# The framework's reordering is switched off around a kernel's own instruction planner

## The chip, the cores and the metric

The kernel runs on one core of one Trainium2 chip. The core has five engines with a queue of instructions each: TensorE (PE, matrix products and transposes; PEld in the profile is its weight load), VectorE (DVE), ScalarE (ACT), GpSimd (POOL) and SyncE (SP, which here only issues DMAs). Each engine runs its queue in the order in which the program holds it and stops where an instruction waits for another engine or for a DMA. The metric is the device time of one execution in microseconds, as the median over several runs.

## The reference, cut to what matters

Two layers of an encoder over 512 tokens of width 1024. Each layer has four steps, and after each a LayerNorm over the residual:

```python
for i in range(DEPTH):                      # DEPTH = 2
    y = swiglu(x, ffn_w_gate[i, 0], ffn_w_up[i, 0], ffn_w_down[i, 0])
    x = layer_norm(ALPHA * x + 0.5 * y, ln_g[i, 0], ln_b[i, 0])
    if i % 2 == 0:
        y = mixer_ab(x, ...)                # 8 heads full attention, 8 heads windowed with a sink
    else:
        y = mixer_c(x, ...)                 # 16 heads, 2-D neighbourhood attention with a bias table
    x = layer_norm(ALPHA * x + y, ln_g[i, 1], ln_b[i, 1])
    y = memory_attn(x, mem, ...)            # 4 heads of 256 into 256 memory tokens
    x = layer_norm(ALPHA * x + y, ln_g[i, 2], ln_b[i, 2])
    y = swiglu(x, ffn_w_gate[i, 1], ffn_w_up[i, 1], ffn_w_down[i, 1])
    x = layer_norm(ALPHA * x + 0.5 * y, ln_g[i, 3], ln_b[i, 3])
```

`swiglu` is `(silu(x @ w_gate) * (x @ w_up)) @ w_down` with a hidden width of 2816. All weights are float32, 217 MB read in all.

## The kernel before

**Products.** Every float32 operand is split into a high part (a cast to fp32r, on ACT) and a low part (the difference, on DVE): `split` (line 293). A product is then three matmuls, high by high, high by low and low by high: `mm3` (line 304). A weight piece of 128 x 1024 thus costs one DMA into a `raw` buffer (two of them), a cast on ACT and a subtraction on DVE into `slab` buffers (27 of them), and only then can PE use it. In the FFN, `down_fast` (line 505) saves one of eight products by sums and differences of blocks on DVE.

**Stages.** `run` (line 190) goes through eight steps: FFN 0, mixer A/B, memory attention, FFN 1, FFN 2, mixer C, memory attention, FFN 3. The activations stay in SBUF: `x` as four tiles of 128 tokens, and transposed and split as `xh` and `xl`, made by `to_features` (line 378: PE transposes into PSUM tiles `t`, ACT casts, DVE subtracts). PSUM tiles have the tags `a` (3), `d` (2) and `t` (3).

**The first FFN** begins by tokens: `ffn_by_tokens` (line 462) loads the first 128 tokens, transposes them, loads gate and up weights of 256 columns in halves, and does 48 matmuls of 256 columns for each token block, 24 into `a` (gate) and 24 into `d` (up). Between them it sets a condition: `self.nc.after = self.nc.ops[-1], {"scalar", "vector"}` (line 467) makes what ACT and DVE do on these weights wait, in the plan, for the last operation of `to_features(0)`. Similar conditions stand for SP's DMAs of side data: the masks `band` and `near` and the 16 `bias` tables (`bias_tables`, line 902, each a DRAM-to-DRAM copy of 128 KB) come after the last DMA of the first group of FFN 0 and FFN 1 (line 588), and the gains, rotary tables and sink of mixer A/B after the last DMA of FFN 0 (line 689). A condition of this kind is known to the planner alone; it is no dependency in the program.

**The planner.** `Graph` (line 64) stands in place of the engines while the kernel is written down: `record` (line 128) keeps each operation with its engine, its cost by a formula (`cost`, line 110) and the operations that it depends on. `emit` (line 165) then plays the program through: each engine has a clock, a heap of operations that will be ready and one of those that are; the operation that can start first is emitted, among the ready ones of an engine the one that was recorded first, and ACT and DVE ("patient") may wait a little for an earlier one. Tiles are granted in the order of recording as buffers come free. The real instruction is issued at that moment:

```python
            _, _, op = heapq.heappop(ready[e])
            op.call()
```

(lines 231 and 232). Line 140 makes that call, so all instructions have line 140 in the profile.

**The framework.** The instructions so emitted go to the framework's tile context (`tile.TileContext`, line 1283). On leaving the context it orders each engine's instructions anew: by its own estimate of times it lets an instruction that is ready pass one that is not, with the order of emission as the priority. It also places tiles in buffers and sets the semaphores.

Of the kernel before, what the change touches and what calls it, by code (L numbers as in the profile page):

```python
# [249 lines left out]
class Kernel:  # L250
# [939 lines left out]
    def run(self, phases=8):  # L1190
        nc, a = self.nc, self.a
        self.ident = self.tile(self.cst, [P, P], F32, "ident")
        make_identity(self.tc.nc, self.ident)
        self.xh = self.tile(self.big, [P, KB, S], F32R, "xh")
        self.xl = self.tile(self.big, [P, KB, S], F32R, "xl")
        self.x = []
        for t in range(NT):
            self.x.append(self.tile(self.big, [P, D], F32, f"x{t}"))
        self.nhalf = self.tile(self.cst, [P, 8], F32, "nhalf")
        nc.gpsimd.memset(self.nhalf, -0.5)  # L1200
        self.junk = self.tile(self.cst, [P, D], BF16, "junk")
        steps = [
            lambda last: self.ffn(0, 0, last, self.masks),
            lambda last: self.mixer_ab(1, last),
            lambda last: self.memory(0, 2, last),
            lambda last: self.ffn(1, 3, last, self.bias_tables),
            lambda last: self.ffn(2, 4, last),
            lambda last: self.mixer_c(5, last),
            lambda last: self.memory(1, 6, last),
            lambda last: self.ffn(3, 7, last),  # L1210
        ]
        for i in range(phases):
            steps[i](i == phases - 1)
        nc.emit()


@with_exitstack
# [69 lines left out]
```

## Time and profile before

| | us |
|---|---|
| median of three runs | 2249.43 (2248.94 to 2249.74) |
| profiled execution, its own time | 2250.06 |
| span of the profiled execution, first to last instruction | 2248.3 |

The page of the profile was taken from one execution. It names engines as above; line numbers are those of the kernel, and tiles have the names of the program without their numbers. In the rows of groups and of the timeline stands what an instruction writes and reads, its shape, how often, how long, and in brackets or behind the bar how long its engine stood idle before it and what ended that. In a row of a stretch (`from:to`) stand its length and then the busy time of each engine with the count of instructions.

### The profile page before, as it was taken

The page shows a single profiled execution, that of the slowest core. Times are in us where ns is not written, and L with a number is a line of the kernel's source. Part 1 is how long each engine was busy: PE and PEld are TensorE (multiplying, and loading weights), DVE is VectorE, ACT ScalarE, POOL GpSimd, SP SyncE. Part 2 cuts the span into 40 slices and gives each one's busy share as a digit, 9 for nine tenths or more (in the row PEclk, how much of TensorE's full clock was granted, in tenths as well). Part 3 has the DMA queues.
Part 4 walks back from the last instruction along what each step waited for, and adds up shares of the span by engine and source line. Part 5 has one row for each costly group of instructions (what it writes and reads, how often), then busy time and mean ns, then how long its engine had stood idle before and what let it go on. Part 6 is the DMA issues. An engine that isn't in the chain of part 4 may idle for free. (4 is left out here: it accounts for less than half of the span.)

```text
span 2248.3 us, 28157 instructions
## 1 busy us (share of the span) xinstructions
PE 2207.0 (98%) x11312; PEld 1871.7 (83%) x11312; DVE 1420.1 (63%) x2116; ACT 882.7 (39%) x1418; POOL 287.0 (13%) x391
## 2 busy tenths in 40 slices
PE   8999999999999999999999999999999999999998
PEld 7888888778898888888888888888888988888886
DVE  5666646788745766665655667368776457666653
ACT  4323332566433433333333333256554434333331
POOL 0000203543000100001100003013411001000011
PEclk9999999999999999999999999999999999999999
DMA  6333241003333332225312334212233333322241
GB/s 207 129 120 113 67 154 57 20 20 90 124 106 113 113 113 90 72 83 168 105 40 86 113 117 150 75 62 68 69 113 96 129 113 113 113 82 72 85 137 38
DMA packets 168755, 221.09 MB, mean 98 GB/s; under 512 B 6192, under 2 KB 136880, under 8 KB 168624
## 3 DMA queue, kind: packets, MB, share of 16 engines
q1 hardware_dynamic: 165552, 208.80, 28.9%
q0 software_dynamic: 3072, 10.49, 1.3%
q8 instruction: 89, 1.46, 0.3%
q14 instruction: 42, 0.34, 0.1%
HBM read 217.17 MB, written 4.19 MB: 98 GB/s over the span
## 5 line engine op out<-in xcount | busy, mean ns | idle before, releaser
L140 PE MATMUL a<-xh,slab 128*128 128x512 f32 (+1 forms) x2960 | 890.8, 382 | 0.0
L140 PEld LDWEIGHTS a<-xh,slab 128*128 128x128 f32 x2960 | 549.1, 188 | 107.1
L140 PE MATMUL d<-slab,slab 128*128 128x512 f32 (+2 forms) x2432 | 572.5, 384 | 4.7 <-DVE slab L140 2.8
L140 PE MATMUL a<-xl,slab 128*128 128x512 f32 (+1 forms) x1480 | 565.0, 382 | 0.0
L140 PEld LDWEIGHTS d<-slab,slab 128*128 128x128 f32 x2432 | 441.1, 188 | 94.3 <-DVE slab L140 4.2
L140 ACT CAST slab<-raw 128x1024 fp32r<-128x1024 f32 x316 | 320.7, 1050 | 310.9 <-DMA raw<-ffn_w_gate 129.8
L140 DVE TENSOR_TENSOR slab<-raw,slab 128x1024 fp32r<-128x1024 f32 x316 | 391.6, 1254 | 72.9 <-ACT slab L140 55.4
L140 PEld LDWEIGHTS a<-xl,slab 128*128 128x128 f32 x1480 | 278.3, 188 | 53.0
L140 DVE TENSOR_TENSOR slab<-slab,slab 128x1024 fp32r<-128x1024 f32 (+2 forms) x208 | 241.4, 1184 | 18.9 <-ACT slab L140 17.6
L140 ACT CAST slab<-slab 128x1024 fp32r<-128x1024 f32 (+1 forms) x144 | 140.1, 1000 | 238.4 <-DVE slab L140 238.3
L140 ACT CAST slab<-t 128x512 fp32r<-128x512 f32 (+3 forms) x261 | 143.5, 572 | 225.9 <-DVE t L140 142.0
L140 PE MATMUL a<-slab,slab 128*128 128x256 f32 (+3 forms) x1336 | 204.9, 303 | 6.2 <-DVE slab L140 2.6
L140 DVE TENSOR_TENSOR slab<-a,t 128x512 f32<-128x512 f32 x56 | 38.7, 691 | 269.3 <-PE a L140 269.3
L140 PEld LDWEIGHTS a<-slab,slab 128*128 128x128 f32 x1336 | 180.6, 194 | 21.5 <-DVE slab L140 6.0
L140 DVE TENSOR_TENSOR slab<-t,slab 128x512 fp32r<-128x512 f32 (+3 forms) x261 | 164.3, 654 | 42.7 <-ACT slab L140 41.5
L140 DVE SCALAR_TENSOR_TENSOR x<-d,x 128x512 f32<-128x512 f32 x216 | 147.3, 685 | 48.3 <-PE d L140 47.3
L140 PE MATMUL t<-slab,slab 128*128 128x512 f32 (+1 forms) x648 | 152.1, 379 | 0.0
L140 ACT ACTIVATE t<-a 128x512 f32<-128x512 f32 (+2 forms) x104 | 57.4, 552 | 225.2 <-PE a L140 203.0
L140 POOL TENSOR_TENSOR x<-x,slab 128x512 f32<-128x512 f32 x24 | 46.0, 1950 | 780.7 <-DVE x L140 780.7
L140 PEld LDWEIGHTS t<-slab,slab 128*128 128x128 f32 x648 | 115.7, 188 | 25.0 <-DVE slab L140 2.2
L140 POOL TENSOR_TENSOR t<-t,l 128x256 f32<-128x256 f32 (+2 forms) x104 | 80.1, 785 | 308.4 <-DVE l L140 308.4
L140 PE MATMUL a<-slab,xh 128*128 128x256 f32 (+1 forms) x432 | 98.1, 319 | 4.1 <-ACT xh L140 4.0
(97 smaller groups left out, 1810.0 us busy)
## 6 DMA issues: line engine op xcount, KB each, us to landing
raw<-ffn_w_gate SPq DMA_DIRECT2D x40, 1024.0 KB
raw<-ffn_w_up SPq DMA_DIRECT2D x40, 1024.0 KB
slab<-ffn_w_down SPq DMA_DIRECT2D x64, 512.0 KB
raw<-ffn_w_down SPq DMA_DIRECT2D x12, 1024.0 KB
raw<-mem_w_kv SPq DMA_DIRECT2D x8, 1024.0 KB
raw<-mem_w_kv SPq DMA_DIRECT2D x16, 512.0 KB
raw<-mem_w_q SPq DMA_DIRECT2D x8, 1024.0 KB
raw<-mem_w_o SPq DMA_DIRECT2D x8, 1024.0 KB
```

What stands on the lines that cost most here:

```text
L140: op.call = lambda: fn(*args, **kw)
```

## The change

Leaving the reordering out for everything that the planner emits: `manual_schedule` is the framework's context in which it keeps each engine's instructions in the order in which they are issued to it. Tiles, dependencies and semaphores are still the framework's. No operation is added, removed or changed.

```diff
@@ -1211,7 +1211,8 @@
         ]
         for i in range(phases):
             steps[i](i == phases - 1)
-        nc.emit()
+        with self.tc.manual_schedule():
+            nc.emit()
```

## The prediction

> **What bounds the kernel now.** The page comes first: which engine is busy over the whole span, and whether its clock is held back.
>
> ```profile
> span 2248.3 us, 28157 instructions
> PE 2207.0 (98%) x11312; PEld 1871.7 (83%) x11312; DVE 1420.1 (63%) x2116; ACT 882.7 (39%) x1418; POOL 287.0 (13%) x391
> PEclk9999999999999999999999999999999999999999
> ```
>
> TensorE (PE) works for 2207.0 of 2248.3 us at full granted clock, so only 41.3 us of the span are not its own work. The change adds and removes no instruction: it can win part of those 41.3 us, or make them more. The next view is the busy time by stretches (PE's first, then weight load, DVE, ACT, POOL, clock, DMA share, GB/s), cut where the idle time sits.
>
> ```profile
> 7.80:11.80 4.00, 0.00 (x0) 0.00 (x0) 2.94 (x3) 3.08 (x5) 0.00 (x0) 1.00 1.13 342
> 14.20:16.90 2.70, 2.69 (x13) 2.69 (x14) 0.66 (x1) 0.29 (x1) 0.00 (x0) 1.00 1.05 231
> 18.40:21.30 2.90, 2.90 (x26) 2.90 (x26) 0.00 (x0) 0.38 (x1) 0.00 (x0) 1.00 1.09 349
> 40.00:300.00 260.00, 260.00 (x1155) 214.88 (x1154) 167.31 (x196) 92.72 (x112) 12.73 (x8) 1.00 0.33 108
> 420.00:620.00 200.00, 191.89 (x1110) 162.08 (x1109) 158.19 (x358) 123.08 (x271) 65.88 (x107) 0.99 0.24 68
> 620.00:1480.00 860.00, 858.20 (x4230) 724.85 (x4229) 522.01 (x659) 299.54 (x411) 68.60 (x74) 1.00 0.31 101
> 1480.00:1740.00 260.00, 251.55 (x1563) 221.92 (x1562) 190.84 (x381) 145.14 (x305) 67.15 (x114) 0.99 0.27 86
> 1740.00:2222.00 482.00, 480.76 (x2433) 408.66 (x2432) 278.73 (x359) 166.40 (x236) 27.90 (x26) 1.00 0.30 99
> 2222.00:2249.00 27.00, 15.53 (x69) 12.53 (x67) 14.77 (x24) 4.97 (x8) 7.33 (x8) 0.88 0.29 78
> ```
>
> The long FFN stretches have nothing to give: 0 us idle in 40 to 300, 1.8 in 620 to 1480, 1.2 in 1740 to 2222. Four places remain: the start, the first token mixer with the memory attention's beginning (200 - 191.9 = 8.1 us), the second mixer (260 - 251.6 = 8.4 us), and the last 27 us, where the final LayerNorms and the output run one after another (11.5 us). The list of PE's waits (total, times, longest) says on whom it waited.
>
> ```profile
> PE t L140 <- DMA x<-x: 6.9, 2, 5.8
> PE a L140 <- ACT xh L140: 4.0, 1, 4.0
> PE t L140 <- DVE x L140: 3.1, 4, 1.2
> PE d L140 <- DVE slab L140: 2.8, 8, 0.7
> PE a L140 <- DVE slab L140: 2.6, 3, 1.2
> PE t L140 <- DVE slab L140: 2.5, 6, 0.6
> ```
>
> Two long waits belong to the start (5.8 us for the first DMA of x, 4.0 us for the cast xh). All others are short, none in these rows over 1.2 us.
>
> **How much order there is to change.** The program of before numbers its instructions as the planner emitted them, and runs them in another order. Laid side by side, from that program alone, 718 of 11312 matmuls stand elsewhere (394 by more than two places), 867 of 1956 DVE instructions (85), 414 of 1220 on ACT (42), and 158 of 299 DMAs on SP, up to 96 places. PE, which sets the time, thus keeps 94% of its order; its moved matmuls lie in the first 40 us and in the two mixers, with a few groups of 10 to 23 in the FFNs.
>
> **The start, the one term with a clear sign.** The timeline of the first 23 us, PE, then ACT, then DVE (start, us, instruction, idle time before it and what ended that):
>
> ```profile
> 5.83 1.94 PE L140 MATMUL t<-ident,x 128*128 128x128 f32 x8 [5.83 <-DMA x<-x]
> 11.81 0.80 PE L140 MATMUL a<-slab,xh 128*128 128x256 f32 x2 [4.04 <-ACT xh L140]
> 14.21 0.90 PE L140 MATMUL t<-ident,x 128*128 128x128 f32 x3 [1.04 <-DMA x<-x]
> 22.07 0.50 PE L140 MATMUL a<-slab,xh 128*128 128x256 f32 x2
> ...
> 7.22 1.04 ACT L140 CAST slab<-raw 128x1024 fp32r<-128x1024 f32 x1 [5.21 <-DMA raw<-ffn_w_gate]
> 8.73 1.04 ACT L140 CAST slab<-raw 128x1024 fp32r<-128x1024 f32 x1 [0.46 <-DMA raw<-ffn_w_gate]
> 10.23 1.04 ACT L140 CAST slab<-raw 128x1024 fp32r<-128x1024 f32 x1 [0.46 <-DMA raw<-ffn_w_up]
> 11.18 1.06 ACT L140 CAST xh<-t 128x512 fp32r<-128x512 f32 x2
> ...
> 9.80 1.23 DVE L140 TENSOR_TENSOR slab<-raw,slab 128x1024 fp32r<-128x1024 f32 x1 [0.28 <-ACT slab L140]
> 12.45 1.28 DVE L140 TENSOR_TENSOR xl<-t,xh 128x512 fp32r<-128x512 f32 x2
> 13.65 1.21 DVE L140 TENSOR_TENSOR slab<-raw,slab 128x1024 fp32r<-128x1024 f32 x1
> ```
>
> PE has the transposed x at 5.83 + 1.94 = 7.8 us, but ACT casts three weight pieces first and comes to xh at 11.18; the matmuls start at 11.81. The planner holds the weight pieces of ACT and DVE behind the split of the first token block (the condition of line 467); the framework knows nothing of that condition. In the planner's order ACT takes xh at once. Its pair takes 1.06 us; it ends at 8.4 if only its second half is left at 7.8, at 8.9 if the whole pair is. The first weight cast follows (1.04: 9.45 to 9.9), then DVE's subtraction (1.23: 10.7 to 11.2), and from there, 10.95 in the middle, PE has a stream. The other three pieces follow at DVE's 1.2 us each and end near 14.6, as now (13.65 + 1.21 = 14.9); PE needs the last of them for the last quarter of the block's 48 matmuls, later than that.
>
> The 13 matmuls of 14.2 to 16.9 took 0.21 us each, the 26 from 18.4 on 0.11. If the slow pace again lasts 2.7 us, 47 matmuls from 10.95 end at 13.65 + 34 x 0.11 = 17.4; if it lasts until 16.9, at 16.9 + 19 x 0.11 = 19.0. Block 1 then needs four transposes (0.5), a cast (0.53) and a hand-over (0.26 or so): its first matmul at 18.7 to 20.3 against 22.07 now. Gain 1.8 to 3.4 us; I take 2.5. The bounds: 0 if ACT still comes late to xh, and 4.04 + 1.04 = 5.1 us if all idle time after the first transposes went. PE is without a gap from 40 to 300 us, so what is won here stays won, unless weights run short; the next part prices that.
>
> The Trainium skill ("TensorE: Matmul & The Clock Gate", What's actually happening) says that the array starts at half rate and needs some 3.4 us of sustained work to come to full rate. By that figure, an estimate, 16 matmuls would be slow and the gain about 2.9 instead of 2.5 us; the trace's own slow stretch of 2.7 us after the pause at 13.2 is a little shorter.
>
> **DMA order on SP.** The masks, gains, the sink and the 16 bias tables run far ahead of their planned places now; they go back behind the weights.
>
> ```profile
> 33.03 4.96 SPq L140 DMA_DIRECT2D bias<-rpb_g  x6
> 73.96 0.38 SPq L140 DMA_DIRECT2D raw<-ffn_w_gate  x1
> ...
> SPq L140 <- DVE slab L140: 46.8, 5, 35.9
> ```
>
> The bias tables cost SP 4.96 / 6 = 0.83 us each, 13.2 us for 16. In the planner's order they come in one row in the second FFN (`ffn(1)`), after its first group. What hides them: SP stands up to 35.9 us waiting for DVE to release a raw buffer, and the DMA engines are 33% busy in 40 to 300. I cost them at nothing. Were that cover gone, the next weight load would come 13.2 us later and PE would stop for up to that. The gains and masks move towards their users, the mixers, which start some 300 us later. Taken away from the first 40 us, they leave room to the weights, which PE does not wait for. Nothing again; bounds 0 to +13.2.
>
> **The mixers.** Here the trace cannot show the other order, so both ends are bounded. At best the planner's order removes all 8.1 + 8.4 = 16.5 us of idle time. At worst each head loses a step that is now covered; the rows that price a step:
>
> ```profile
> L140 ACT CAST slab<-t 128x512 fp32r<-128x512 f32 (+3 forms) x261 | 143.5, 572 | 225.9 <-DVE t L140 142.0
> L140 DVE TENSOR_TENSOR slab<-t,slab 128x512 fp32r<-128x512 f32 (+3 forms) x261 | 164.3, 654 | 42.7 <-ACT slab L140 41.5
> ```
>
> A transposed tile is split by a 0.57 us cast and a 0.65 us subtraction, 1.2 us together; 16 heads and 8 pairs make 24 x 1.2 = 29 us. I take 0: both orders are fixed lists for engines that serve them in turn, most differences on DVE and ACT are swaps of neighbours, and PE's waits there are of the length of one such step, which either order leaves somewhere.
>
> **The tail.** LayerNorm is a chain through DVE, ACT and POOL; no order shortens it. 0.
>
> **Sum.** The profiled execution took 2250.06 us beside its span of 2248.3. 2250.06 - 2.5 = 2247.6. The median of the runs (2249.43) is 0.6 lower: 2246.9 us.
>
> **The rivals.** *Faster:* the mixers give back half of their idle time, 8.3 us, besides the start: 2249.4 - 2.5 - 8.3 = 2238.6. For it: these waits end on DVE's and ACT's slab, which an order can bring forward. Against it: PE keeps nearly all its order there.
>
> *Slower:* the head of a queue blocks. In the mixers the next instruction by the plan is not ready when PE or DVE comes to it (a softmax tile still on ACT or POOL), and what stands behind it may not pass; the framework had pulled such work forward, groups of up to 64 places on PE. Half of the 24 steps uncovered: 14.6 us, 2249.4 - 2.5 + 14.6 = 2261.5. It decides from the third such step on, since two (2.4 us) only eat the gain of the start. For it: DVE is 79% busy in 420 to 620 (158.19 of 200) and has little room. Against it: that a block on DVE reaches PE only when PE's own cover of a few us is used up.
>
> The Trainium skill ("PSUM — Partial Sum Buffer", Engine vs sequencer instructions) states that the queues of ScalarE, VectorE and GpSimdE are strict first-in-first-out. It speaks for this rival, and by it the 14.6 us are paid wherever the head is late. The trace agrees: ACT stood idle 0.46 us before its cast at 10.23, for weights, while x, transposed since 7.8, stood behind that cast.
>
> *The change does little:* the framework's priorities already follow the emission, and the same waits return: 2249.4.
>
> *Weights late on SP,* as priced: 2249.4 - 2.5 + 13.2 = 2260.1.
>
> **How the numbers follow.** This kernel's runs tell a change from none at about 0.2%, 4.5 us. Forecast 0.42 (own range 2243 to 2251; 0.04 of it below 2244.9), little change 0.08, faster rival 0.27, blocked queues 0.20, weights late 0.03. Faster: 0.27 + 0.04 = 0.31. Same: 0.38 + 0.08 = 0.46. Slower: 0.23. The range goes from the start plus three quarters of the mixers' idle time (2249.4 - 2.5 - 12.4 = 2234.5, so 2235) to the blocked queues' 2262, leaving out the far half of that rival, the late weights and the end of the faster one.
>
> **What would show it.** Right: the cast xh starts before the weight casts, before 8.5 us; PE's wait for xh falls from 4.0 to under 2.5 us, and block 1's first matmul comes at 18.7 to 20.3; idle PE time in the two mixers stays within 3 us of 16.5; the bias DMAs stand in one row after 700 us with no PE wait for a slab behind them. Wrong: PE's idle time in the mixers over 20 or under 12 us, a longer stretch than 0.5 us idle inside the FFNs, or a start whose gain is gone by 300 us.

## The result, and the profile after

| | before | after |
|---|---|---|
| median of four runs, us | 2249.18 (2248.68 to 2249.74) | 2260.97 (2260.05 to 2263.3) |
| ratio | | 1.0054, 95% interval 1.0036 to 1.0071 |
| profiled execution: its time, us | 2250.06 | 2260.05 |
| its span, us | 2248.3 | 2258.3 |

The change makes the kernel 0.54% slower, beyond the 0.2% that can be told from no change. The forecast was 2246.9; the time is that of the rival with blocked queues (2261.5).

The page of the kernel after, span and busy engines:

```profile
span 2258.3 us, 28099 instructions
PE 2201.9 (98%) x11312; PEld 1871.6 (83%) x11312; DVE 1426.2 (63%) x2116; ACT 878.9 (39%) x1418; POOL 293.5 (13%) x391
```

The same 11312 matmuls, in 10.0 us more span, and PE is busy 5.1 us less (2201.9 against 2207.0): 15.1 us more without work. The same stretches as before (length, then PE, PEld, DVE, ACT, POOL, clock, DMA share, GB/s):

```profile
7.80:11.80 4.00, 1.70 (x6) 1.30 (x6) 3.58 (x5) 3.83 (x5) 0.00 (x0) 1.00 1.14 343
40.00:300.00 260.00, 260.00 (x1152) 215.12 (x1151) 171.35 (x198) 92.25 (x113) 13.72 (x8) 1.00 0.31 104
420.00:620.00 200.00, 189.03 (x1092) 159.75 (x1093) 156.47 (x354) 121.13 (x268) 68.19 (x107) 0.99 0.22 64
620.00:1480.00 860.00, 857.33 (x4230) 725.42 (x4229) 523.30 (x657) 298.97 (x412) 71.15 (x74) 1.00 0.31 104
1480.00:1740.00 260.00, 240.32 (x1497) 212.90 (x1496) 187.36 (x379) 140.81 (x301) 64.10 (x114) 0.99 0.25 80
1740.00:2222.00 482.00, 480.34 (x2472) 410.86 (x2472) 283.86 (x359) 170.09 (x241) 29.44 (x26) 1.00 0.31 103
```

Between 7.8 and 11.8 us PE has work now where it had none. The FFN stretches are as full as before. The mixers are not: 200 - 189.0 = 11.0 us idle (8.1 before) and 260 - 240.3 = 19.7 (8.4 before). The list of PE's waits (total, times, longest) names the cause of most of it:

```profile
PE t L140 <- DVE slab L140: 14.4, 9, 1.9
PE t L140 <- DVE x L140: 6.1, 9, 2.3
...
PE a L140 <- ACT slab L140: 4.2, 3, 1.9
```

The 4.0 us wait for the cast `xh` is gone. New is the first row: before it was 2.5 us in 6 waits of at most 0.6.

Windows shift when a kernel runs late, so the account below counts matmuls instead: the time at which each kernel starts its n-th matmul, less the time of before (us, worked out from the profiled execution of each; 1700 is in FFN 0, 2960 behind the first mixer, 7400 ahead of the second, 8400 near its end). The last column is the difference of the spans. The labels are those of the experiments.

```
n (time before)   1700 (372.7)  2960 (611.7)  7400 (1497.2)  8400 (1664.4)  span
after                 -1.8          +2.5          +2.3          +10.1       +10.0
e1_act_dve            +3.7          +5.8          +5.3           +4.7        +5.8
e2_pe_sp_pool         +2.1         +11.0         +17.7          +20.1       +22.4
e3_bank_plan          -0.9          +0.2          -0.3           -5.8        -6.8
e4_bank_plan_auto     +1.1          +9.1          +8.9           +8.4        +6.7
e5_bank_c             -1.5          +4.2          +4.1           -1.7        -2.7
e6_bank_rest          -1.7          +1.1          +0.6          +10.1       +10.1
e7_keys_once          -0.8          +2.9          +2.7           +1.5        +2.0
e8_bank_keys          -1.3          +1.5          +1.0           -3.6        -2.9
e9_table              -1.6          +2.1          +1.8           +9.4        +9.3
e10_bank_table        -1.5          -0.4          -0.8           -7.4        -7.8
```

So, in these executions, the change wins 1.8 us at the start, loses 4.3 in the first mixer, nothing in FFN 1 and 2, loses 7.8 in the second mixer, and nothing after it.

How far single executions can be trusted is seen where kernels run the same order. Laid side by side from the traces, PE's matmuls up to the 7400th stand in one order in after, e5 and e7, and in one order in e3, e6 and e8. Over the first mixer (from 1700 to 2960) the first three lose 4.3, 5.7 and 3.7 us, the other three 1.1, 2.8 and 2.8. A part of this is the granted clock, which dips at other places in each execution. The same 12 us inside the first mixer, in e5 and in e7 (the clock is the figure before the last two):

```profile
590.00:602.00 12.00, 9.17 (x52) 8.43 (x50) 8.64 (x13) 4.51 (x8) 1.83 (x2) 0.72 0.28 87
590.00:602.00 12.00, 8.50 (x66) 7.65 (x65) 10.18 (x16) 6.34 (x12) 1.83 (x2) 1.00 0.33 98
```

Before and after have 0.86 here, e3 has 1.00. A clock of 0.72 over 12 us leaves out 3.4 us of full clock, 0.86 leaves out 1.7 (estimates from these rows); the traces' clock records have it at a half for 6.8 us in e5 and for 3.4 us in before and after. Differences of up to 2 us between single executions of this table are therefore not clear of noise. The 7.8 us of the second mixer are clear of it: e6, with the same order of matmuls there as after, loses 9.5, and its clock dipped in that mixer (0.89 in 1560 to 1575 us, 1.00 in after).

**The start.** The timeline of PE, then ACT, then DVE of the kernel after (start, us, instruction, idle time before it and what ended that):

```profile
9.53 0.58 PE L140 MATMUL a<-slab,xh 128*128 128x256 f32 x1 [1.62 <-ACT slab L140]
...
17.74 0.38 PE L140 MATMUL d<-slab,xh 128*128 128x256 f32 x1 [0.88 <-DVE slab L140]
...
20.42 0.51 PE L140 MATMUL a<-slab,xh 128*128 128x256 f32 x2
...
7.09 0.59 ACT L140 CAST xh<-t 128x512 fp32r<-128x512 f32 x1 [5.08 <-PE t L140]
...
8.43 2.94 ACT L140 CAST slab<-raw 128x1024 fp32r<-128x1024 f32 x3
11.39 1.28 ACT L140 ACT_TABLE_LOAD   x1
15.11 0.38 ACT L140 ACTIVATE t<-a 128x256 f32<-128x256 f32 x1 [2.44 <-PE a L140]
15.39 1.04 ACT L140 CAST slab<-raw 128x1024 fp32r<-128x1024 f32 x1
...
16.46 1.23 DVE L140 TENSOR_TENSOR slab<-raw,slab 128x1024 fp32r<-128x1024 f32 x1 [3.45 <-ACT slab L140]
```

ACT takes `xh` at 7.09 and PE has its first product at 9.53 instead of 11.81. Block 1 starts at 20.42 (22.07 before). The fourth weight cast stands at 15.39, behind the Silu, which ACT reaches early, loads a table for (1.28 us) and then waits 2.44 us for; DVE's subtraction follows, and PE stands 0.88 us for it.

**The second mixer, one head pair.** `keys` (line 952) has ACT copy and DVE subtract from one PSUM tile, for two heads `s` and two halves. The kernel after, ACT, DVE and PE:

```profile
1611.63 1.17 ACT L140 CAST slab<-t 64x512 fp32r<-64x512 f32 x2 [3.19 <-PE t L140]
1613.55 0.58 ACT L140 CAST slab<-t 64x512 fp32r<-64x512 f32 x1 [0.75 <-DVE slab L140]
1614.89 1.68 ACT L140 CAST slab<-t 64x512 fp32r<-64x512 f32 x3 [0.75 <-DVE slab L140]
...
1612.84 0.68 DVE L140 TENSOR_TENSOR slab<-t,slab 64x512 fp32r<-64x512 f32 x1 [1.30 <-ACT slab L140]
1614.17 0.68 DVE L140 TENSOR_TENSOR slab<-t,slab 64x512 fp32r<-64x512 f32 x1 [0.65 <-ACT slab L140]
1615.50 4.19 DVE L140 TENSOR_TENSOR slab<-t,slab 64x512 fp32r<-64x512 f32 x6 [0.65 <-ACT slab L140]
...
1614.82 0.39 PE L140 MATMUL d<-xh,slab 128*128 128x512 f32 x1
1617.05 0.63 PE L140 MATMUL t<-ident,t 128*128 128x128 f32 x4 [1.84 <-DVE slab L140]
1617.43 0.48 PE L140 MATMUL d<-xh,slab 128*128 128x512 f32 x1
```

The same place in the kernel before:

```profile
1604.03 1.17 ACT L140 CAST slab<-t 64x512 fp32r<-64x512 f32 x2 [2.66 <-PE t L140]
1605.94 2.29 ACT L140 CAST slab<-t 64x512 fp32r<-64x512 f32 x4 [0.75 <-DVE slab L140]
...
1605.22 0.68 DVE L140 TENSOR_TENSOR slab<-t,slab 64x512 fp32r<-64x512 f32 x1 [0.68 <-ACT slab L140]
1606.56 4.76 DVE L140 TENSOR_TENSOR slab<-t,slab 64x512 fp32r<-64x512 f32 x7 [0.65 <-ACT slab L140]
...
1607.61 0.39 PE L140 MATMUL d<-xl,slab 128*128 128x512 f32 x1
1608.02 1.25 PE L140 MATMUL t<-ident,t 128*128 128x128 f32 x8
```

In the kernel after, ACT and DVE hand the tile to and fro: ACT stands 0.75 us for DVE and DVE 0.65 us for ACT, in turn, each through the other's one instruction (0.68 and 0.58 us). ACT's third copy needs nothing that DVE makes; it reads the tile that PE filled, and another half of it than the subtraction before it. It waits because in the built program two engines' uses of one PSUM tile exclude each other by semaphores, reads too. The planner counts a dependency only where one of the two writes (`if over and (w or writes)` in `record`), so its list sets the copies and subtractions side by side. Engines that keep to that list take them one by one, with the splits of the transposed tiles queued behind. Those splits free the PSUM tiles `t` late, and PE, with four transposes at the head of its queue, waits 1.84 us, while the query products (`d<-xh,slab`) stand ready behind them. ACT and DVE take three turns each here, five hand-overs. Before, the framework let ACT's last two copies go in one row, three hand-overs, and PE did two more products first; its waits of this kind were at most 0.6 us. From 1505 to 1672 us PE's waits of this kind are, in the kernel after:

```profile
PE t L140 <- DVE slab L140: 12.9, 7, 1.9
```

and in the kernel before:

```profile
PE t L140 <- DVE slab L140: 1.3, 3, 0.6
```

Seven waits of about 1.84 us, in a mixer of eight head pairs.

### The profile page after: what moved, and what is told of

Its sections match the earlier page's. It is cut to its first block, busy times and chain, and to the rows that moved or that the text cites. A ratio compares the mean times of both kernels' runs of the same rounds, so it can differ in the third digit from the quotient of the medians.

```text
span 2258.3 us, 28099 instructions
## 1 busy us (share of the span) xinstructions
PE 2201.9 (98%) x11312; PEld 1871.6 (83%) x11312; DVE 1426.2 (63%) x2116; ACT 878.9 (39%) x1418; POOL 293.5 (13%) x391
## 4 chain that ended last, share of the span: by engine, by line
PE 88%; DVE 5%; ACT 4%; POOL 2%; issue 1%; DMA 0%; POOLq 0%; ACTq 0%; DVEq 0%
PE a L140 52%; PE d L140 24%; PE t L140 12%; DVE slab L140 3%; ACT slab L140 2%; DVE x L140 1%; DVE t L140 1%; POOL lny L140 1%; ACT t L140 1%; ACT junk L140 1%; ACT xh L140 0%; POOL rms8y L140 0%; POOL slab L140 0%; DVE mn L140 0%; DMA x<-x 0%
```

## Experiments

**Is it the engines' order, or PE's?** Two runs fix the order of some engines only; the framework goes on ordering the others. The edit of e1; in e2 the set is PE, SP and Pool.

```diff
-        with self.tc.manual_schedule():
+        with self.tc.manual_schedule(engines={mybir.EngineType.Activation, mybir.EngineType.DVE}):
             nc.emit()
```

> Only ACT and DVE keep the planner's order; PE, SP and POOL are reordered as before. Theory (the loss sits in the order of ACT and DVE: a PSUM tile read by both is handed to and fro, and what stands behind it in the two queues is blocked): the second mixer (1480 to 1740 us) has again PE waits of 1.8 us for a transposed tile, once a head pair, and the start keeps its gain of 1.7 us; 2256 to 2261 us. Rival (PE's or SP's fixed order does it): 2247 to 2251 us.

Measured 2255.97, ratio 1.0025 (1.0016 to 1.0035). The time lies at the lower edge of what was expected (2256), but for another reason, so theory and time agree by luck: the second mixer's waits of 1.8 us are absent, and it loses nothing (+5.3 to +4.7 in the account). ACT and DVE still hand the tile to and fro there, with the same stands of 0.75 and 0.65 us. Most of the loss sits at the start, whose gain is gone. There the framework pulled the transposes of later blocks of x ahead of the first products, and PE stood for their DMAs. PE's waits in this kernel, the first row over the whole span, the second in its second mixer (1502 to 1670 us):

```profile
PE t L140 <- DMA x<-x: 12.5, 3, 6.4
...
PE t L140 <- DVE slab L140: 0.4, 1, 0.4
```

> The complement: PE, SP and POOL keep the planner's order, ACT and DVE are reordered as before. Theory: the 1.8 us waits in the second mixer are gone, its PE idle time is near the 8.4 us of before; the start loses its gain; 2248 to 2253 us. Rival (PE's or SP's fixed order does it): 2257 to 2262 us.

Measured 2272.37, ratio 1.0097 (1.0083 to 1.011): a miss, and the worst of all. The 1.8 us waits are gone, as the theory had it, but the 4.0 us wait for `xh` is back, the boundaries at the LayerNorms lose, and so does each mixer. PE's waits in this kernel, the last row in its second mixer (1514 to 1686 us):

```profile
PE t L140 <- DVE x L140: 14.3, 11, 2.6
...
PE a L140 <- ACT xh L140: 4.0, 1, 4.0
...
PE t L140 <- DVE slab L140: 4.3, 9, 0.8
```

What follows from both: the 1.8 us waits need ACT and DVE in the planner's order and PE's queue head blocked besides. An order fixed on some engines, with the others ordered by another plan, was slower than the framework's whole order in both runs; than the planner's whole order (2260.97) one was slower (e2) and one faster (e1).

**Does the planner's missing dependency cause them?** The planner counts every use of one PSUM tile by two engines as dependent, whatever part of it they use, with the change (e3) and with the framework's reordering left on (e4):

```diff
-                over = opens or p0 < a1 and a0 < p1 and (
-                    info["bank"] and q.engine != engine or any(...)
-                )
-                if over and (w or writes) and q is not op:
+                share = info["bank"] and q.engine != engine
+                over = opens or share or p0 < a1 and a0 < p1 and any(...)
+                if over and (w or writes or share) and q is not op:
```

> As the change, all engines in the planner's order, but the planner also counts two engines' uses of one PSUM tile as dependent, reads too, so that it plans other work between them. Theory: the seven waits of 1.8 us fall under 0.6 us, the second mixer's PE idle time from 19.7 to under 10 us, and the time to 2243 to 2250 us. Rival (the hand-over is not the cause, or the planner loses as much by the stricter rule): 2257 us and more.

Measured 2244.08, ratio to before 0.9973 (0.9963 to 0.9983): 16.9 us under the changed kernel and faster than before. The second mixer's stretch, ACT and DVE at the same keys, and PE's wait in that mixer (1495 to 1660 us):

```profile
1480.00:1740.00 260.00, 253.52 (x1613) 226.87 (x1613) 193.53 (x384) 146.81 (x309) 61.58 (x114) 0.99 0.28 92
...
1602.03 2.27 ACT L140 CAST slab<-t 64x512 fp32r<-64x512 f32 x4 [2.91 <-PE t L140]
...
1603.23 5.45 DVE L140 TENSOR_TENSOR slab<-t,slab 64x512 fp32r<-64x512 f32 x8 [1.31 <-ACT slab L140]
...
PE t L140 <- DVE slab L140: 1.4, 1, 1.4
```

ACT does all four copies in one row and DVE its subtractions after them: one hand-over. Of the seven waits one is left, of 1.4 us where under 0.6 was expected, and PE's idle time in the stretch is 6.5 us (under 10 expected). The second mixer is 5.5 us shorter than before (-0.3 to -5.8). Not all of that is idle time: between the 7400th and the 8400th matmul PE stands 3.8 us before and 1.6 in e3; the other 3.3 us are shorter busy time, at a clock of 1.00 in both, and why is open.

> The same stricter planner with the framework's reordering on, as in the kernel before. Theory: the framework already lets ready work pass a blocked head, so little changes: 2246 to 2251 us. Rival (the stricter rule is by itself a better or worse plan): outside 2244 to 2254 us.

Measured 2256.96, ratio 1.0031 (1.0019 to 1.0042): a miss, slower than before. The better list gains nothing in the second mixer once the framework has reordered it (8.9 to 8.4), and the first mixer loses 8 us (1.1 to 9.1). So the rule pays only where its order is kept. Why the first mixer suffers so was not followed up.

**In which part?** The strict rule only while mixer C, step 5, is written down (e5), and everywhere but there (e6, `i != 5`):

```diff
+            nc.strict = i == 5
             steps[i](i == phases - 1)
```

> The change with the planner's stricter PSUM rule in the second mixer alone. Theory (the second mixer loses by the hand-over between ACT and DVE, the first mixer's loss is a separate 4 us): PE's wait for transposed tiles in the second mixer falls from 12.9 to under 3 us, the first mixer stays 4 us behind before; 2245 to 2249 us. Rival (the gain with the rule everywhere came from elsewhere): 2254 us and more.

Measured 2248.9, ratio 0.9993 (0.9984 to 1.0002), as expected: the first mixer still loses (-1.5 to +4.2), the second gains 5.8 (4.1 to -1.7), and PE waits there once for a transposed tile, 1.4 us.

> The complement: the stricter rule everywhere but in the second mixer. Theory: the seven waits of 1.8 us in the second mixer stay, the first mixer gains about 3 us, the start loses about 1; 2256 to 2261 us. Rival: 2250 us and less.

Measured 2259.8, ratio 1.0043 (1.003 to 1.0057), in the range. PE's waits in this kernel from 1505 to 1672 us are those of the changed one (line 141 is its line 140, as a line was added above):

```profile
PE t L141 <- DVE slab L141: 12.9, 7, 1.9
```

The second mixer's loss is undone by the rule there and not by the rule elsewhere. In the first mixer 2.8 us are lost with the rule (-1.7 to +1.1) where after lost 4.3, which is not clear of what one order shows (3.7 to 5.7); 3 us less were expected. Nor does the rule cost anything at the start: e3 and e6 run PE's first 1686 matmuls in the order of after, and e6 gains 1.7 us there. The 1 us that e3 seemed to lose is the execution's.

**The hand-overs alone.** The changed kernel with the planner as it was, and only `keys` written otherwise: ACT reads the PSUM tile for its own halves in one row and makes the other halves from its own result in SBUF, then DVE subtracts. One hand-over in place of five, the same numbers of copies and subtractions.

```diff
-                for half in (own, other):
-                    nc.scalar.copy(h[half], ps[own])
+                nc.scalar.copy(h[own], ps[own])
+            for s, (h, l) in enumerate(ks[pair]):
+                own, other = slice(64 * s, 64 * s + 64), slice(64 - 64 * s, 128 - 64 * s)
+                nc.scalar.copy(h[other], h[own].bitcast(F32))
```

> The change, planner untouched; only the key split of the second mixer is written so that ACT reads the PSUM tile twice, back to back, and makes its other two copies from its own results in SBUF, so that the tile goes to DVE once and not to and fro. Theory: the 1.8 us waits of PE go below 0.6 us with no other part of the order changed; 2247 to 2253 us. Rival (it is the blocked queue by itself, whatever the tile): the waits stay over 1.2 us, 2257 us and more.

Measured 2251.18, ratio 1.0005 (0.9996 to 1.0014), as expected. PE's waits in this kernel from 1505 to 1672 us:

```profile
PE t L140 <- DVE slab L140: 4.1, 7, 0.6
```

Still seven, but a third as long: the second mixer now gains 1.2 us (2.7 to 1.5) where the changed kernel lost 7.8. This is the cleanest proof of the mechanism: the planner's rules are untouched, and PE's order in the second mixer is that of after but for 10 matmuls, so it is the hand-overs and not another order on PE that made the waits long.

> Both together, the stricter rule everywhere but in the first FFN, where it cost 1 us of the start's gain, and the key split with one hand-over. If the two causes add up: 2239 to 2244 us, start as in the change (block 1 at 20.4 us), second mixer's PE idle time under 7 us. If the two remove the same wait: 2242 to 2246 us.

With the strict rule besides (from step 1 on): 2247.23, ratio 0.9988 (0.9979 to 0.9997), a miss on both sides. The two cures don't add: the second mixer gains 4.6 us (1.0 to -3.6), no more than the 5.5 of the rule alone. The 1 us at the start that this run was to win back had never been lost (see e6).

**The first mixer.** The changed kernel there, PE and ACT:

```profile
425.32 0.73 PE L140 MATMUL a<-slab,slab 128*128 128x512 f32 x2 [0.88 <-ACT t L140]
...
431.81 0.50 PE L140 MATMUL d<-slab,slab 128*128 128x512 f32 x1 [1.04 <-ACT slab L140]
...
423.20 1.28 ACT L140 ACT_TABLE_LOAD   x1 [1.65 <-DVE mn L140]
```

ACT's first Exp after Silu loads a function table, 1.28 us, which `cost` leaves out; PE's next score product is planned that much too early. The planner is told of it (`op.table` holds the function where it is Exp or Silu), for the changed kernel (e9) and for e3's (e10):

```diff
+            if op.table and op.table[0] != table:
+                table = op.table[0]
+                t += 1280.0
             now[e] = t + op.ns
```

> The changed kernel; the planner alone is told that ACT loads a new function table (1.28 us) whenever it goes from Silu to Exp or back, which its cost formula leaves out. Theory T: part of the 4.3 us that the change loses at the first mixer, and what it lost at the start at 16.9 us, are waits at PE's queue head for an ACT result that comes 1.28 us later than planned. Then PE's 0.88 us wait for ACT at 425 us is filled, the first mixer loses about 1 us less, the seven waits of 1.8 us in the second mixer stay, and the time is 2258.5 to 2260.2. Rival U: the table load is only one of many small errors and another wait takes its place: 2260.2 to 2262.

Measured 2258.99, ratio 1.0042 (1.0029 to 1.0054). The same two waits in this kernel:

```profile
425.47 1.40 PE L140 MATMUL a<-slab,slab 128*128 128x512 f32 x4 [0.44 <-ACT t L140]
...
431.93 0.51 PE L140 MATMUL d<-slab,slab 128*128 128x512 f32 x1 [0.81 <-ACT slab L140]
```

They are shorter (0.88 to 0.44, 1.04 to 0.81) but not filled; in e5 and e7, which run the order of after, they are 0.87 to 0.89 and 1.04, so this is no noise. The time is in the range of theory T, but its interval overlaps that of the change (1.0036 to 1.0071), and the 3.7 us that the first mixer loses are what e7 loses there with the order of after. That leaving the table load out of the plan lengthens these two waits is shown; what it costs the kernel is not clear of noise.

> The kernel whose planner counts reads of one PSUM tile by two engines as dependent (2244.08 us), and the planner told of the 1.28 us table loads besides. Theory T: PE's waits for ACT of 1.1 and 1.7 us at 427 and 434 us shrink by about 1.3 us together: 2241.5 to 2243.3. Rival U: other waits take their place: 2243.3 to 2246.

Measured 2241.25, ratio 0.9963 (0.9949 to 0.9976), 0.25 us under the range of theory T; the fastest kernel here, 8.4 us under the 2249.69 that before took beside it. Of the two waits of 1.1 and 1.7 us the second is gone and the first is 0.9:

```profile
427.01 1.40 PE L140 MATMUL a<-slab,slab 128*128 128x512 f32 x4 [0.90 <-ACT t L140]
```

Its interval overlaps that of e3, and the first mixer as a whole loses 1.1 us in both (-0.9 to +0.2; -1.5 to -0.4), e3 at a clock without a dip there. That it beats before is shown, and that it beats e3 is likely only.

## Why the prediction was wrong

**What bounds the kernel: right.** PE's work is the span, and only the start, the mixers and the tail had anything to give or to lose.

**The start: right in mechanism, mis-sized.** The cast came at 7.09 (said: before 8.5), PE's wait for it went from 4.0 us to nothing in the list, and its first stream began at 10.79 (said: 10.7 to 11.2). Two windows of the kernel after show the pace from there:

```profile
10.80:13.50 2.70, 2.70 (x12) 2.70 (x13) 2.21 (x2) 1.85 (x2) 0.00 (x0) 1.00 1.09 256
13.50:16.80 3.30, 3.30 (x26) 2.99 (x24) 0.34 (x1) 1.32 (x2) 0.00 (x0) 1.00 1.04 227
```

12 matmuls in 2.7 us, then 26 in 3.3, though the clock column shows 1.00 in both: in this execution the slow stretch lasted about 2.7 us from the stream's beginning, as the first of the two cases had it. In e7, which runs the same order here, it went on to about 16.5 us, nearly as the second case had it:

```profile
13.50:16.80 3.30, 3.30 (x17) 3.30 (x17) 0.00 (x0) 0.74 (x2) 0.00 (x0) 1.00 1.03 227
```

The traces hold no clock record ahead of 13.7 us in after and 16.7 us in e7, so the 1.00 before that is no measurement. Which of the two cases comes is the execution's, not the order's, and the gain at the 1700th matmul is 0.8 us in e7 and 1.8 in after. The Trainium skill ("TensorE: Matmul & The Clock Gate", What's actually happening) gives some 3.4 us to full rate; counted from the stream's beginning after shows less (2.7 us) and e7 more (some 5.7). The prediction's estimate by that figure comes to 3.0 us rather than 2.9: 22.07 less 10.95 + 3.4 + 31 x 0.11 + 1.29. Block 1 came at 20.42 in after, not at 18.7 to 20.3, a gain of 1.65 us and not 2.5. The working had the four weight casts in a row; the plan put the Silu between the third and the fourth, and the 2.44 us that ACT stood for it became PE's 0.88.

**DMA order on SP at nothing: right.** The account is flat from matmul 2960 to 7400 (+2.5 to +2.3). The 16 bias copies stand in one row, in the kernel after:

```profile
769.41 11.33 SPq L140 DMA_DIRECT2D bias<-rpb_g  x16
```

They took 0.71 us each, and the FFN stretch around them is as full as before (2.7 us idle in 620 to 1480, 1.8 before).

**The mixers at nothing: the step that failed.** "I take 0: both orders are fixed lists for engines that serve them in turn, most differences on DVE and ACT are swaps of neighbours, and PE's waits there are of the length of one such step, which either order leaves somewhere." The differences are indeed swaps of neighbours, and they were taken as small for that. But in `keys` the neighbours are four readers of one tile, whose uses exclude each other: the order decides between one hand-over and five, at 0.65 to 0.75 us each. The step left out that the planner's list was drawn up without that exclusion; the framework's reordering left three hand-overs of the five, in before and in e2. The condition was there to be read in `record`; the trace of before showed a 0.75 us stand of the same kind as well. With the account's terms the sum is 2250.06 - 1.8 + 4.3 + 7.8 = 2260.4, against 2260.05 for the profiled execution, from which these terms were taken. The sign "idle in the mixers over 20 us" came out: 11.0 + 19.7 = 30.7.

**The rivals.** *Slower* was right in place and in deciding point, and near in price: 12 steps of 1.2 us were 14.6, and 12.1 were lost (4.3 + 7.8), most of it in seven waits of 1.84, past the third. That the totals lie so close is luck in part, since fewer steps of a longer kind made it up. It was right in kind too, PE's queue head blocked with ready products behind. It named the wrong tile: not a softmax tile but the key split's PSUM tile in the second mixer; in the first, a softmax tile on ACT (0.88 us) is one of several. Its counter-argument, that PE's cover would take up a block on DVE, did not hold: the cover ended 1.84 us too early, seven times. *Faster* did not come with the list as it stood. e3 and e10 come nearer to its time (2244.1 and 2241.3) once the planner knows what the program enforces, but hardly by its mechanism: PE stands 17.5 us in the two mixers' stretches in e3 and 13.9 in e10, against 16.5 before, and most of their gain lies in PE's shorter busy time (2198.8 and 2201.3 us against 2207.0). *Weights late* did not come.

The Trainium skill ("PSUM — Partial Sum Buffer", Engine vs sequencer instructions) states that the queues of ScalarE, VectorE and GpSimdE are strict first-in-first-out, and this was the rule that spoke for the slower rival. The trace agrees: the splits behind the blocked copies passed nothing on ACT and DVE. PE's queue did likewise here: its ready products stood 1.84 us behind its transposes.

**Still open:** the larger part of the first mixer's loss. PE's idle time between the 1700th and the 2960th matmul, which the clock disturbs less, is 8.1 us before; 12.3, 12.4 and 13.1 in after, e5 and e7; 12.1 to 12.2 with the strict rule (e3, e6, e8); 11.3 with the table loads planned (e9), and 10.4 with both (e10). So the strict rule does little or nothing here, and the table loads explain perhaps 1 us. The rest is spread over waits of about 1 us on POOL, ACT and DVE, and no one cause was isolated.

## What to carry to other kernels

Before a planner's order is made binding, compare its rules of dependency with the waits that the program really holds: a list that ignores one exclusion was mended in part by the framework's reordering here, and cost 7.8 us in one mixer without it. Price a swap by what it does to the chain of hand-overs between two engines, not by how far an instruction moves. Do not expect half of a plan to bring half of its effect: an order fixed on some engines meets others that are moved by another plan (e2, 2272.4; e1, 2256.0; all fixed, 2261.0; none, 2249.2). And run one order more than once before a difference of 1 or 2 us between two traces is explained.

## What the runs showed that was not expected

- Fixing three of the engines (e2, +22.4 us of span) is worse than fixing five (+10.0) or two (+5.8). The effects of the engines do not add.
- Two engines that only read one PSUM tile take turns in this program: 0.75 us of ACT's time and 0.65 us of DVE's at each hand-over, for copies of 0.58 and subtractions of 0.68 us. Each stand is the other engine's instruction and some 0.07 us more (0.75 - 0.68, 0.65 - 0.58), though from ACT's third copy on none of these needs what the one before it on the other engine writes.
- PE's busy time for the same 11312 matmuls is not a constant: 2207.0 us before, 2201.9 after, 2198.8 in e3 and 2201.3 in e10. Idle time of a window therefore overstates what a stretch loses (+11.2 us idle in the second mixer's window, 7.8 us lost), and the n-th matmul's start is the safer measure of that, though it takes in the dips of the clock in its execution.
